# A weighted sum of two expert outputs: the 8-token tile moved from the end to the start, the last store in two halves

## The chip, the cores and the metric

The kernel runs on one core of one Trainium2 chip. The metric is the device time of one execution in microseconds; the time of a kernel is the median of several executions. A profiled execution also has a span, from the first to the last instruction of the program that the profiler recorded.

The core's engines that matter here are VectorE (DVE in the profile), ScalarE (ACT) and SyncE (SP), each with its own instruction stream. Data moves between HBM and the on-chip memory (128 partitions) by 16 DMA engines. A DMA is issued by SP or by ACT; the profile shows the two queues as q1 (SP) and q10 (ACT). Each of the 16 engines takes its share of every DMA, and a DMA has landed when all of them have reported.

## The reference

For 16 x 1024 tokens there are two expert outputs of 512 float32 each, and two weights. The result is their weighted sum.

```python
batch, seq, hidden, n_experts, k = 16, 1024, 512, 8, 2
expert_outputs: (batch, seq, k, hidden) float32      # 67.1 MB
combine_weights: (batch, seq, k) float32             # 0.13 MB

weights = combine_weights[..., np.newaxis]
return np.sum(expert_outputs * weights, axis=2)      # (batch, seq, hidden), 33.6 MB
```

## The kernel before

The 16384 tokens are dealt to the 128 partitions, 128 tokens to each (`per`). They are handled in 11 tiles: ten of J = 12 tokens per partition and a last one of LAST = 8. The helper `rows` (L34 to L38) splits the token axis into two blocks. In the first, each partition owns 120 tokens that lie one after the other in HBM, so that its rows start 480 KB apart in the input. In the second, each partition owns 8 tokens, with rows 32 KB apart (4 KB a token). `eo`, `cw` and `o` are functions that give the input, the weights and the output of `c` tokens from token `t` on.

All weights stay on chip in `wt`, loaded by two DMAs on ACT's queue (L54 to L57): 120 tokens first, then 8. An activation on a constant (L60) loads ACT's table early.

The loop (L62) goes over the 11 tiles. Each takes one of four buffers `et` of 12 tokens x 2 x 512 float32 per partition, 48 KB. The result `ot` (L65) lies in the first half of the same buffer, so a buffer is free for a later load once its store has landed. Loads (L69) are all issued by SP, one DMA per tile. Tile 0 alone is loaded in two pieces, 2 tokens and then the rest, the first of them in rows of 4 KB.

There are three kinds of tiles:

- Tiles 0 to 8: one product on DVE over both experts with the weights broadcast (L78), one sum on DVE (L79), and a store of 12 tokens issued by ACT (L80).
- Tile 9: ACT scales the first expert's half token by token (L86), DVE multiplies the second expert's half at once (L101) and adds (L102). SP issues the store (L103).
- Tile 10, the one of 8 tokens: for each token ACT scales the first expert's half (L86) and DVE multiplies and adds the second one's (L90), so that the two engines go hand in hand. SP issues the store of all 8 tokens (L103).

No semaphore is written by hand. A framework finds the dependencies between instructions from the parts of the tiles that they touch, sets the waits, and decides on the order of each engine's instructions. In the trace of before, SP issues the load of tile 10 at 194.63 us, ahead of the store of tile 9 at 218.73 us, though the loop names them the other way round.

Of the kernel before, what the change touches and what calls it, by code (L numbers as in the profile page):

```python
# [1 line left out]

# [4 lines left out]


@with_exitstack
def kernel(  # L10
    ctx: ExitStack,
    tc: tile.TileContext,
    expert_outputs: bass.AP,
    combine_weights: bass.AP,
    out: bass.AP,
):

    nc = tc.nc  # L20
    b, s, k, h = expert_outputs.shape
    assert k == 2
    n = b * s
    P = nc.NUM_PARTITIONS
    per = n // P
    assert per * P == n
    J, LAST = 12, 8
    main = per - LAST
    assert main % J == 0
    eo = expert_outputs.rearrange("b s k h -> (b s) (k h)")  # L30
    cw = combine_weights.rearrange("b s k -> (b s) k")
    o = out.rearrange("b s h -> (b s) h")

    def rows(x):  # L34

        a = x[0 : P * main, :].rearrange("(p t) f -> p t f", p=P)
        b = x[P * main : n, :].rearrange("(p t) f -> p t f", p=P)
        return lambda t, c: a[:, t : t + c, :] if t < main else b[:, t - main : t - main + c, :]  # L38

    eo, cw, o = rows(eo), rows(cw), rows(o)  # L40

    dt = mybir.dt.float32
    mult = mybir.AluOpType.mult
    add = mybir.AluOpType.add
    copy = mybir.ActivationFunctionType.Copy

    last = main // J

    wpool = ctx.enter_context(tc.tile_pool(name="w", bufs=1))
    ipool = ctx.enter_context(tc.tile_pool(name="in", bufs=4))  # L50

    wt = wpool.tile([P, per * k], dt)

    for t, c in ((0, main), (main, LAST)):  # L54
        nc.scalar.dma_start(
            out=wt[:, k * t : k * (t + c)].rearrange("p (t k) -> p t k", k=k), in_=cw(t, c)
        )  # L57

    warm = wpool.tile([P, 1], dt)
    nc.scalar.activation(out=warm, in_=nc.const_aps.tensor(1.0, (P, 1), dt), func=copy)  # L60

    for g in range(last + 1):  # L62
        et = ipool.tile([P, J, k * h], dt)

        ot = et.rearrange("p j f -> p (j f)")[:, 0 : J * h].rearrange("p (j f) -> p j f", f=h)  # L65
        t0, c = g * J, J if g < last else LAST

        for a, m in ((0, 2), (2, c - 2)) if g == 0 else ((0, c),):
            nc.sync.dma_start(  # L69
                out=et[:, a : a + m],  # L70
                in_=eo(t0 + a, m),
                max_dma_last_dim=k * h * 4 if g + a == 0 else None,
            )
        if g < last - 1:

            wb = wt[:, g * J * k : (g + 1) * J * k].unsqueeze(2).to_broadcast([P, J * k, h])
            ek = et.rearrange("p j (k h) -> p (j k) h", k=k)
            nc.vector.tensor_tensor(out=ek, in0=ek, in1=wb, op=mult)  # L78
            nc.vector.tensor_tensor(out=ot, in0=et[:, :, 0:h], in1=et[:, :, h : 2 * h], op=add)  # L79
            nc.scalar.dma_start(out=o(t0, c), in_=ot)  # L80
            continue


        for i in range(c):
            t = t0 + i
            nc.scalar.activation(  # L86
                out=et[:, i, 0:h], in_=et[:, i, 0:h], func=copy, scale=wt[:, 2 * t : 2 * t + 1]
            )
            if g == last:
                nc.vector.scalar_tensor_tensor(  # L90
                    out=ot[:, i, :],
                    in0=et[:, i, h : 2 * h],
                    scalar=wt[:, 2 * t + 1 : 2 * t + 2],
                    in1=et[:, i, 0:h],
                    op0=mult,
                    op1=add,
                )
        if g < last:
            w1 = wt.rearrange("p (t k) -> p t k", k=k)[:, t0 : t0 + c, 1:2]
            x1 = et[:, :, h : 2 * h]  # L100
            nc.vector.tensor_tensor(out=x1, in0=x1, in1=w1.to_broadcast([P, c, h]), op=mult)  # L101
            nc.vector.tensor_tensor(out=ot, in0=et[:, :, 0:h], in1=x1, op=add)  # L102
        nc.sync.dma_start(out=o(t0, c), in_=ot[:, 0:c])  # L103


# [1 line left out]
_INS = ['expert_outputs', 'combine_weights']  # L107
_OUTS = [((16, 1024, 512), 'float32')]


# [23 lines left out]
```

## Time and profile before

| | us |
|---|---|
| median of 5 runs | 239.1 |
| lowest and highest of the runs | 239.02, 240.06 |
| the profiled execution | 239.86 |
| its span | 238.1 |
| DVE busy | 194.0 (81% of the span) |
| ACT busy | 14.0 (6%) |

HBM is read for 67.24 MB and written for 33.55 MB, 423 GB/s over the span. The main groups of instructions (line, engine, operation, tiles, shapes, count | busy us, mean ns of one | idle time of the engine just before them, with what ended it):

```profile
L78 DVE TENSOR_TENSOR et<-et,wt 128x12288 f32<-128x12288 f32 x9 | 116.6, 12956 | 26.8 <-DMA et<-in_expert_outputs_dram 26.8
L79 DVE TENSOR_TENSOR et<-et 128x6144 f32<-128x6144 f32 x9 | 59.0, 6558 | 0.3
L86 ACT ACTIVATE et<-et,wt 128x512 f32<-128x512 f32 x20 | 12.5, 709 | 211.0 <-DMA et<-in_expert_outputs_dram 211.0
L90 DVE SCALAR_TENSOR_TENSOR et<-et,wt 128x512 f32<-128x512 f32 x8 | 5.6, 746 | 3.9 <-ACT et L86 3.7
```

The first line reads: line 78 ran nine times on VectorE, 12.956 us each; before these instructions VectorE was idle for 26.8 us in all, and each of those waits was ended by a load. The idle time of ACT is that of an engine with work in the last two tiles only.

The DMA issues (tiles, issuing queue, count, KB each, median us from issue to landing):

```profile
et<-in_expert_outputs_dram SPq DMA_DIRECT2D x9, 6144.0 KB, 31.7
out_dram<-et ACTq DMA_DIRECT2D x9, 3072.0 KB, 32.6
et<-in_expert_outputs_dram SPq DMA_DIRECT2D x1, 5120.0 KB, 16.8
et<-in_expert_outputs_dram SPq DMA_DIRECT2D x1, 4096.0 KB, 26.9
out_dram<-et SPq DMA_DIRECT2D x1, 3072.0 KB, 13.7
out_dram<-et SPq DMA_DIRECT2D x1, 2048.0 KB, 9.1
```

The time to landing holds the wait behind earlier transfers as well as the transfer.

### The profile page before, as it was taken

How to read it: one execution, taken by the hardware profiler on the slowest of the kernel's cores; microseconds unless marked ns; L12 is line 12 of the kernel's file. 1: busy time of each engine (PE TensorE's matmuls, PEld its weight loads, DVE VectorE, ACT ScalarE, POOL GpSimd, SP SyncE). 2: the span in 40 equal slices, each digit the busy share in tenths (PEclk: the TensorE clock that was granted, in tenths of full speed). 3: DMA queues.
4: the chain of work that ended last, by engine and by line, in shares of the span. 5: the costliest groups of instructions: out<-in, count | busy, mean ns of one | idle time of the engine just before them, and what ended most of it. 6: DMA issues, size and time to landing. Idle time of an engine off the chain costs nothing.

```text
span 238.1 us, 154 instructions
## 1 busy us (share of the span) xinstructions
DVE 194.0 (81%) x28; ACT 14.0 (6%) x22; POOL 0.2 (0%) x4
## 2 busy tenths in 40 slices
DVE  0009999999999999999699969969996999687630
ACT  2000000000000000000000000000000000660700
POOL 0000000000000000000000000000000000000000
DMA  8999999999999999999999999899999999999996
GB/s 308 441 463 396 396 529 392 392 446 413 405 396 462 438 417 458 401 516 405 462 396 405 429 429 504 351 462 396 524 396 462 396 405 454 399 462 434 405 428 259
DMA packets 3728, 100.80 MB, mean 423 GB/s; under 512 B 528, under 2 KB 656, under 8 KB 912
## 3 DMA queue, kind: packets, MB, share of 16 engines
q1 hardware_dynamic: 2144, 72.35, 70.7%
q10 hardware_dynamic: 1584, 28.44, 27.9%
HBM read 67.24 MB, written 33.55 MB: 423 GB/s over the span
## 4 chain that ended last, share of the span: by engine, by line
DMA 60%; DVE 33%; ACT 2%; DVEq 0%; ACTq 0%; issue 0%; SPq 0%
DMA et<-in_expert_outputs_dram 32%; DMA out_dram<-et 28%; DVE et L78 22%; DVE et L79 11%; ACT et L86 2%; DVE et L90 1%; DVEq L129 0%; ACTq L129 0%; SPq L69 0%; DVEq L78 0%; ACTq L86 0%
## 5 line engine op out<-in xcount | busy, mean ns | idle before, releaser
L78 DVE TENSOR_TENSOR et<-et,wt 128x12288 f32<-128x12288 f32 x9 | 116.6, 12956 | 26.8 <-DMA et<-in_expert_outputs_dram 26.8
L79 DVE TENSOR_TENSOR et<-et 128x6144 f32<-128x6144 f32 x9 | 59.0, 6558 | 0.3
L86 ACT ACTIVATE et<-et,wt 128x512 f32<-128x512 f32 x20 | 12.5, 709 | 211.0 <-DMA et<-in_expert_outputs_dram 211.0
L90 DVE SCALAR_TENSOR_TENSOR et<-et,wt 128x512 f32<-128x512 f32 x8 | 5.6, 746 | 3.9 <-ACT et L86 3.7
L101 DVE TENSOR_TENSOR et<-et,wt 128x6144 f32<-128x6144 f32 x1 | 6.6, 6557 | 2.3 <-DMA et<-in_expert_outputs_dram 2.3
L102 DVE TENSOR_TENSOR et<-et 128x6144 f32<-128x6144 f32 x1 | 6.6, 6557 | 0.9 <-ACT et L86 0.9
L60 ACT ACT_TABLE_LOAD x1 | 1.3, 1283 | 1.7 <-PEq L118 1.7
L60 ACT ACTIVATE warm<-const-float32-1.0 128x1 f32<-128x1 f32 x1 | 0.2, 204 | 0.0
L118 POOL MEMSET const-bfloat16-1.0<- 128x1 bf16 x1 | 0.1, 102 | 0.0
L118 POOL MEMSET const-uint8-127<- 128x1 uint8 x1 | 0.1, 102 | 0.0
L118 POOL MEMSET const-float32-0.0<- 128x1 f32 x1 | 0.1, 99 | 0.2 <-issue 0.2
L118 POOL MEMSET const-float32-1.0<- 128x1 f32 x1 | 0.1, 99 | 0.0
## 6 DMA issues: line engine op xcount, KB each, us to landing
et<-in_expert_outputs_dram SPq DMA_DIRECT2D x9, 6144.0 KB, 31.7
out_dram<-et ACTq DMA_DIRECT2D x9, 3072.0 KB, 32.6
et<-in_expert_outputs_dram SPq DMA_DIRECT2D x1, 5120.0 KB, 16.8
et<-in_expert_outputs_dram SPq DMA_DIRECT2D x1, 4096.0 KB, 26.9
out_dram<-et SPq DMA_DIRECT2D x1, 3072.0 KB, 13.7
out_dram<-et SPq DMA_DIRECT2D x1, 2048.0 KB, 9.1
et<-in_expert_outputs_dram SPq DMA_DIRECT2D x1, 1024.0 KB, 5.1
wt<-in_combine_weights_dram ACTq DMA_DIRECT2D x1, 120.0 KB, 3.2
```

Source lines behind the costliest of these rows:

```text
L60: nc.scalar.activation(out=warm, in_=nc.const_aps.tensor(1.0, (P, 1), dt), func=copy)
L78: nc.vector.tensor_tensor(out=ek, in0=ek, in1=wb, op=mult)
L79: nc.vector.tensor_tensor(out=ot, in0=et[:, :, 0:h], in1=et[:, :, h : 2 * h], op=add)
L86: nc.scalar.activation(out=et[:, i, 0:h], in_=et[:, i, 0:h], func=copy, scale=wt[:, 2 * t : 2 * t + 1])
L90: nc.vector.scalar_tensor_tensor(out=ot[:, i, :], in0=et[:, i, h : 2 * h], scalar=wt[:, 2 * t + 1 : 2 * t + 2], in1=et[:, i, 0:h], op0=mul ...
L101: nc.vector.tensor_tensor(out=x1, in0=x1, in1=w1.to_broadcast([P, c, h]), op=mult)
L102: nc.vector.tensor_tensor(out=ot, in0=et[:, :, 0:h], in1=x1, op=add)
L118: nc = _bacc.Bacc("TRN2", target_bir_lowering=False, num_devices=1)
```

## The change

The block of 8 tokens per partition comes first: it is the first 1024 tokens of the input in place of the last, and it is tile 0. Ten tiles of 12 tokens follow. Tile 0 is still loaded in two pieces, now of 2 and 6 tokens. Tiles 0 to 8 keep the two long DVE instructions, over 8 tokens in tile 0. Tile 9 stays as it was. Tile 10, which goes token by token, has 12 tokens, and its result is stored by two DMAs of 6 tokens each, both on SP. The weights of the 8 tokens are loaded ahead of the 120 others.

```diff
-    J, LAST = 12, 8
-    main = per - LAST
-    assert main % J == 0
+    J, FIRST = 12, 8
+    assert (per - FIRST) % J == 0
...
-        a = x[0 : P * main, :].rearrange("(p t) f -> p t f", p=P)
-        b = x[P * main : n, :].rearrange("(p t) f -> p t f", p=P)
-        return lambda t, c: a[:, t : t + c, :] if t < main else b[:, t - main : t - main + c, :]
+        a = x[0 : P * FIRST, :].rearrange("(p t) f -> p t f", p=P)
+        b = x[P * FIRST : n, :].rearrange("(p t) f -> p t f", p=P)
+        return lambda t, c: a[:, t : t + c, :] if t < FIRST else b[:, t - FIRST : t - FIRST + c, :]
...
-    last = main // J
+    last = (per - FIRST) // J
...
-    for t, c in ((0, main), (main, LAST)):
+    for t, c in ((0, FIRST), (FIRST, per - FIRST)):
...
-        t0, c = g * J, J if g < last else LAST
+        c = J if g else FIRST
+        t0 = FIRST + (g - 1) * J if g else 0
 
-        for a, m in ((0, 2), (2, c - 2)) if g == 0 else ((0, c),):
+        for a, m in ((0, c),) if g else ((0, 2), (2, c - 2)):
             nc.sync.dma_start(
                 out=et[:, a : a + m],
                 in_=eo(t0 + a, m),
-                max_dma_last_dim=k * h * 4 if g + a == 0 else None,
+                max_dma_last_dim=None if g + a else k * h * 4,
             )
         if g < last - 1:
-
-            wb = wt[:, g * J * k : (g + 1) * J * k].unsqueeze(2).to_broadcast([P, J * k, h])
-            ek = et.rearrange("p j (k h) -> p (j k) h", k=k)
+            wb = wt[:, t0 * k : (t0 + c) * k].unsqueeze(2).to_broadcast([P, c * k, h])
+            ek = et[:, 0:c].rearrange("p j (k h) -> p (j k) h", k=k)
             nc.vector.tensor_tensor(out=ek, in0=ek, in1=wb, op=mult)
-            nc.vector.tensor_tensor(out=ot, in0=et[:, :, 0:h], in1=et[:, :, h : 2 * h], op=add)
-            nc.scalar.dma_start(out=o(t0, c), in_=ot)
+            nc.vector.tensor_tensor(
+                out=ot[:, 0:c], in0=et[:, 0:c, 0:h], in1=et[:, 0:c, h : 2 * h], op=add
+            )
+            nc.scalar.dma_start(out=o(t0, c), in_=ot[:, 0:c])
             continue
...
-        nc.sync.dma_start(out=o(t0, c), in_=ot[:, 0:c])
+        for a, m in ((0, c),) if g < last else ((0, c // 2), (c // 2, c // 2)):
+            nc.sync.dma_start(out=o(t0 + a, m), in_=ot[:, a : a + m])
```

## The prediction

> **What bounds the kernel now.** I read the slices first, then the queues, the order of time, and stretches of the tail. The page's second part is the whole answer in two lines (40 slices of 5.95 us; tenths of the 16 DMA engines, then GB/s):
>
> ```profile
> DMA  8999999999999999999999999899999999999996
> GB/s 308 441 463 396 396 529 392 392 446 413 405 396 462 438 417 458 401 516 405 462 396 405 429 429 504 351 462 396 524 396 462 396 405 454 399 462 434 405 428 259
> ```
>
> Only the first and the last slice are not full. The queues' shares say the same:
>
> ```profile
> q1 hardware_dynamic: 2144, 72.35, 70.7%
> q10 hardware_dynamic: 1584, 28.44, 27.9%
> ```
>
> Together 98.6% of 238.1 us, so 234.8 us of the span the engines move bytes and 3.3 us they don't. The chain of waits gives DVE a third of the span, but that is the early part, where DVE had work piled up while the DMA engines were just as full; no byte waited for it. From 117 us on DVE is idle before each tile until its load lands. In order of time (start, duration, instruction, idle before):
>
> ```profile
> 117.57 12.96 DVE L78 TENSOR_TENSOR et<-et,wt 128x12288 f32<-128x12288 f32 x1 [2.04 <-DMA et<-in_expert_outputs_dram]
> ...
> 139.34 12.96 DVE L78 TENSOR_TENSOR et<-et,wt 128x12288 f32<-128x12288 f32 x1 [2.22 <-DMA et<-in_expert_outputs_dram]
> ...
> 161.11 12.96 DVE L78 TENSOR_TENSOR et<-et,wt 128x12288 f32<-128x12288 f32 x1 [2.22 <-DMA et<-in_expert_outputs_dram]
> ```
>
> The period is 21.77 us for one load and one store of 12 tokens (6144 + 3072 KB, 9.437 MB), 433.5 GB/s. That is my price for bytes: 14.51 us for a load of 12 tokens alone, 9.68 for one of 8; 7.26 for a store of 12 tokens, 4.84 for 8, 3.63 for a half of 12. At that price the 100.8 MB cost 232.5 us, begun at about 2.0 us.
>
> The tail, first the instructions, then stretches (bounds, length, busy of DVE, ACT, POOL, clock, DMA share, GB/s):
>
> ```profile
> 218.73 9.77 SPq L103 DMA_DIRECT2D out_dram<-et  x2
> 221.60 5.01 ACT L86 ACTIVATE et<-et,wt 128x512 f32<-128x512 f32 x8 [9.49 <-DMA et<-in_expert_outputs_dram]
> 222.36 5.77 DVE L90 SCALAR_TENSOR_TENSOR et<-et,wt 128x512 f32<-128x512 f32 x8 [3.65 <-ACT et L86]
> ```
>
> ```profile
> 204.00:212.00 8.00, 6.56 (x1) 7.35 (x12) 0.00 (x0) 1.00 1.06 459
> 212.00:218.70 6.70, 6.55 (x1) 0.11 (x1) 0.00 (x0) 1.00 0.95 411
> 218.70:221.50 2.80, 0.00 (x1) 0.00 (x0) 0.00 (x0) 1.00 0.99 424
> 221.50:228.40 6.90, 5.56 (x8) 5.01 (x8) 0.00 (x0) 1.00 1.04 449
> 228.40:232.40 4.00, 0.00 (x0) 0.00 (x0) 0.00 (x0) 1.00 0.94 403
> 232.40:236.00 3.60, 0.00 (x0) 0.00 (x0) 0.00 (x0) 1.00 0.86 369
> 236.00:238.10 2.10, 0.00 (x0) 0.00 (x0) 0.00 (x0) 1.00 0.02 8
> ```
>
> The last load lands at 221.52 and the last store is issued 6.6 us later, yet the engines stay full: tiles 8 and 9 have stores waiting in the queues, and they cover the last tile's arithmetic. This cover is the quantity that decides the case.
>
> **The change, part by part.** *Bytes.* None is added or taken: 11 loads, 11 stores' worth, two weight loads. Price 0, as long as no DMA engine idles where it didn't.
>
> *Eight tokens first.* Tile 0's load ends at 18.00 now (the chain of waits has it there); 2 MB less at 433.5 GB/s make it 13.2. Its product is 12.957 x 8/12 = 8.64 us, its sum 6.558 x 8/12 = 4.37, so its store goes out at about 26.3 in place of 37.72. Tile 1 lands at 13.2 + 14.5 = 27.7 and DVE waits 1.4 us for it. The engines are full of loads meanwhile (the four buffers would take 23 MB of them, 53 us), so 11.4 us earlier on the store is worth 0: it changes the order of the bytes. Buffer 0 comes free sooner, so the fifth load is issued some 14 us sooner, behind others in its queue: 0.
>
> *The weight loads* are as many, with 8 KB ahead of 120 KB. The 120 KB now travel beside tile 0's load. In the trace the engines are under-used between 2.2 and 3.0 us, while the 120 KB travel ahead; at most 0.3 us can be won there, and at most 0.3 lost by having them later, since 0.12 MB cost 0.28. I take 0.
>
> *SP and ACT queues.* SP issues the ten later loads, then tile 9's store, then two stores where there was one: one DMA issue more (0.35 us by L103's issues), behind a wait that it would not have delayed. Nothing is queued on SP behind the last store. ACT gets 4 more activations in the last tile (12 x 0.709 = 8.5 us), and DVE 4 more L90.
>
> *The last tile, 12 tokens in two stores.* L90 starts 0.84 us after the landing (221.52 to 222.36) and takes 5.77/8 = 0.721 per token. Let X be the landing of the last load. The sixth token ends at X + 0.84 + 6 x 0.721 = X + 5.17, the twelfth at X + 9.49; the halves are issued at X + 5.2 and X + 9.55. What covers them? X is the time of the slowest of 16 engines: by the landing records of the last load now, 15 engines were through at 219.4 to 219.7 and the last at 221.52. Call Y = X - 2.1 the time of the 15. At Y there remain tile 9's store (7.26 us) and a rest r of tile 8's. For r: both queues with work alternate packet by packet, one load's and one store's, hence the common period. The first store's packets begin 3.7 us after its issue now (37.72 to 41.44 by the packets' records); from 26.3 that is 30.0, when tile 2's load, begun at 27.3, is 1.5 of its 8 packets per engine ahead (1.81 us each). Stores then pair with loads one for one, so the loads stay 1.5 packets ahead, 2.3 if tile 1's store comes late (issued 47.3, wanted at 30.0 + 8 x (1.81 + 0.605) = 49.3, with 3.7 to start). So r is 1.5 to 2.3 of 8 packets of tile 8's store, 1.4 to 2.1 us; I take 1.7. The cover is 1.7 + 7.3 = 9.0 us, until Y + 9.0.
>
> From issue to first bytes takes 1.3 us at the kernel's start (issued 0.73, bytes from 2.0) and 3.7 for that first store, whose engines were busy. In the tail the engines run dry, so the near row is the start's. First half: Y + 7.3 + 1.3 = Y + 8.6, 0.4 us inside the cover: no gap. It lasts until Y + 12.6. Second half: Y + 11.65 + 1.3 = Y + 12.95: a gap of 0.35. By the other end, 3.7, the first half starts at Y + 11.0 (gap 2.0) and the second at Y + 15.35 (gap 0.7): 2.7 us. With r = 2.1 and 1.3 no gap is left. So 0 to 2.7, taken as 0.35; and since the slowest engine, which ends the kernel, is behind the others and has less or no gap, I put 0.2 on the end.
>
> *The end of the last store.* Now the other engines are done about 0.9 us before the last (the final 2.1 us hold almost no bytes). Smaller last packets may shorten this: between -0.9 and 0, taken as 0, since the order of packets on that engine doesn't change in kind.
>
> *The 32 KB pitch at the front.* Now loads of this pitch run from about 203 to 219 us, where the stretches above show 459 and 411 GB/s, mean 437: no price. In the first tile the pieces are 2 and 6 tokens of such rows, which no row shows; between 0 and, if it ran at the 308 GB/s of the first slice, 4.19 MB/308 - 9.68 = 3.9 us. I take 0, the row of the same pitch. The Trainium skill has a rule against such pitches ("DMA: Bandwidth & Descriptors", Latency and other measured facts): copies with per-partition pitches of large powers of two slow down, from 512 KiB on in its table, to half at 4 MiB. By its 512 KiB figure (207 against 214) tile 0's load would be an estimated 0.3 us dearer, by its worst one 10 us; 32 KB is below the table, and the stretches above show no loss.
>
> The sum: 0 + 0 + 0.2 + 0. The profiled execution, 238.1 us of span, took 239.86 in all, 1.76 around the span and 0.76 above the median of 239.1; the difference is what I carry over. Span 238.3, **time 239.3 us**.
>
> **Rivals.** *The cover is short* (slower). Place: after tile 9's store in the last 15 us. If a store needs over about 1.9 us from issue to bytes, both halves leave gaps that exceed 0.72 us together: at 2.5 us, the first half begins at Y + 9.8 (0.8), the second at Y + 14.15 (0.7), so +1.5: 240.6. For it: 12 tokens of arithmetic stand where 8 stood, and the first store's 3.7. Against it: that 3.7 contains waiting for busy engines, and the slowest engine has 2 us more of cover.
>
> *The halves don't part*: if the first store waits for all 12 tokens, 3 MB start at Y + 12.95, a gap of 3.95 us: 243. Against it: L90 already starts after one activation of a tile in which eight are to come, so waits follow parts of a tile.
>
> *The order on SP turns*: the last load behind the wait of tile 9's store, issued near 216 in place of 180; the engines would stand idle from about 208, tile 8's store being done, to 217: +9 or more, 248. Now SP puts that load (194.63) ahead of the store (218.73).
>
> *A tidier end* (faster): the 0.9 us of the last engine go, and 0.1 at the start: 238.1. For it: packets at the end are a quarter smaller. Against it: the lag of one engine is in nearly every load's landing.
>
> *A slow pitch at the front*: up to 3.9 us, 243.
>
> **How the numbers follow.** A measurement of this kernel tells 0.3%, 0.72 us, from no change. No change, by my sum: 0.47, with its own range 238.5 to 239.8. Short cover 0.28; halves not parted 0.03; order 0.02; pitch 0.02: slower 0.35. Tidier end: faster 0.18. The range takes in the gain of 0.9 to 1.0 and a cover short by most of the 2.7: 238.0 to 241.4; beyond it lie the three dear rivals and what is left of the short cover.
>
> **What would show it.** Slices of DMA at 9 from the second to the last but one; the first store issued near 26; DVE idle 1 to 2 us before every tile from the second on; the last L90 9.5 us after the last load; the stretch between that landing and the last store's issue above 400 GB/s. I am wrong if that stretch falls under 380, if the two last stores are issued together, or if the shares of the queues, near 234.8 us together, change by more than 0.7 us.

## The result and the profile after

The changed kernel takes 240.5 us in the median of 32 executions (239.35 to 241.33), the kernel before 239.1 (56 executions, 238.99 to 240.62). The ratio is 1.0042, with a 95% interval from 1.0032 to 1.0052: slower by 0.4%. The median moved further (1.4 us) than the ratio (1.0 us), because both kernels have executions in two places about a microsecond apart, a lower group with spans near 237.3 us and an upper one near 238.4, and the change moved most executions from the lower group to the upper one. The spans of the executions show it:

```
                     executions   span, median   span of 238.0 us or more   time minus span
before                   87           237.3              28                      1.78 to 1.80
changed                  32           238.4              26                      2.04
```

(The 87 are the executions of the kernel before that ran beside the experiments below.) So the 1.4 us of the median are 1.1 us of span and 0.26 us outside it. The profiled execution of the kernel before, 239.86 us, was one of the upper group. That of the changed kernel has 240.5 us, 238.4 of them span.

Slices and queues of the changed kernel (tenths of the DMA engines, GB/s; then packets, MB, share):

```profile
DMA  7999989999999999999999999999999999998996
GB/s 278 445 398 528 396 366 514 396 412 425 396 482 392 400 445 458 396 441 433 482 416 404 466 412 421 425 449 425 458 408 474 412 416 458 400 491 371 441 410 270
...
q1 hardware_dynamic: 2288, 73.40, 71.9%
q10 hardware_dynamic: 1584, 27.39, 26.8%
```

The engines are as full as before, 98.7% of the span. But 98.7% of 238.4 are 235.3 us for the same bytes; before they were 234.8 (235.2 and 234.7 by the records of the single packets). A packet is what one of the 16 engines moves at a time, here 48 KB of a load of 12 tokens or 24 KB of its store. The start in order of time:

```profile
13.34 8.69 DVE L77 TENSOR_TENSOR et<-et,wt 128x8192 f32<-128x8192 f32 x1 [13.34 <-DMA et<-in_expert_outputs_dram]
22.07 4.42 DVE L78 TENSOR_TENSOR et<-et 128x4096 f32<-128x4096 f32 x1
26.52 150.27 ACTq L81 DMA_DIRECT2D out_dram<-et  x8
27.85 12.96 DVE L77 TENSOR_TENSOR et<-et,wt 128x12288 f32<-128x12288 f32 x1 [1.36 <-DMA et<-in_expert_outputs_dram]
40.84 6.56 DVE L78 TENSOR_TENSOR et<-et 128x6144 f32<-128x6144 f32 x1
```

Tile 0's load is there at 13.2, its store goes out at 26.52, tile 1's at 47.4. The tail:

```profile
214.47 17.03 SPq L104 DMA_DIRECT2D out_dram<-et  x3
221.96 7.46 ACT L86 ACTIVATE et<-et,wt 128x512 f32<-128x512 f32 x12 [14.11 <-DMA et<-in_expert_outputs_dram]
222.72 8.43 DVE L90 SCALAR_TENSOR_TENSOR et<-et,wt 128x512 f32<-128x512 f32 x12 [8.28 <-ACT et L86]
```

```profile
218.70:221.90 3.20, 0.00 (x0) 0.00 (x0) 0.00 (x0) 1.00 1.07 461
221.90:227.10 5.20, 4.17 (x7) 5.14 (x9) 0.00 (x0) 1.00 1.01 435
227.10:231.20 4.10, 4.04 (x7) 2.32 (x4) 0.00 (x0) 1.00 0.93 399
231.20:234.00 2.80, 0.00 (x0) 0.00 (x0) 0.00 (x0) 1.00 1.02 434
234.00:236.00 2.00, 0.00 (x0) 0.00 (x0) 0.00 (x0) 1.00 0.96 412
```

From the landing of the last load (221.9) over the last token (231.15) to 236 the engines are full in every stretch. No gap opened in the tail. The time was not lost where the change does most to the program.

### The profile page after: what moved, and what is told of

The parts are those of the page before. It is cut to its first block, busy times and chain, and to the rows that moved or that the text cites. A ratio compares the mean times of both kernels' runs of the same rounds, so it can differ in the third digit from the quotient of the medians.

```text
span 238.4 us, 167 instructions
## 1 busy us (share of the span) xinstructions
DVE 190.5 (80%) x32; ACT 16.4 (7%) x26; POOL 0.2 (0%) x4
## 4 chain that ended last, share of the span: by engine, by line
DMA 68%; DVE 26%; ACT 2%; SPq 0%; issue 0%; DVEq 0%; ACTq 0%
DMA et<-in_expert_outputs_dram 44%; DMA out_dram<-et 23%; DVE et L77 16%; DVE et L78 8%; DVE et L90 2%; ACT et L86 2%; SPq L69 0%; DVEq L130 0%; ACTq L130 0%; DVEq L77 0%; ACTq L86 0%
## 5 line engine op out<-in xcount | busy, mean ns | idle before, releaser
L77 DVE TENSOR_TENSOR et<-et,wt 128x12288 f32<-128x12288 f32 (+1 forms) x9 | 112.4, 12484 | 28.7 <-DMA et<-in_expert_outputs_dram 28.7
L78 DVE TENSOR_TENSOR et<-et 128x6144 f32<-128x6144 f32 (+1 forms) x9 | 56.9, 6321 | 0.3
L86 ACT ACTIVATE et<-et,wt 128x512 f32<-128x512 f32 x24 | 14.9, 707 | 211.3 <-DMA et<-in_expert_outputs_dram 211.3
L90 DVE SCALAR_TENSOR_TENSOR et<-et,wt 128x512 f32<-128x512 f32 x12 | 8.2, 746 | 8.5 <-ACT et L86 8.3
L102 DVE TENSOR_TENSOR et<-et 128x6144 f32<-128x6144 f32 x1 | 6.6, 6559 | 0.9 <-ACT et L86 0.9
```

The costliest lines, as they stand in the source:

```text
L78: nc.vector.tensor_tensor(out=ot[:, 0:c], in0=et[:, 0:c, 0:h], in1=et[:, 0:c, h : 2 * h], op=add)
L86: nc.scalar.activation(out=et[:, i, 0:h], in_=et[:, i, 0:h], func=copy, scale=wt[:, 2 * t : 2 * t + 1])
L90: nc.vector.scalar_tensor_tensor(out=ot[:, i, :], in0=et[:, i, h : 2 * h], scalar=wt[:, 2 * t + 1 : 2 * t + 2], in1=et[:, i, 0:h], op0=mul ...
```

## The experiments

Each was run against the kernel before on the same chip. Ratios carry a 95% interval.

**The kernel before again.**

> The kernel before, once more, for its own trace and its spread. Its executions so far lie near 239.05 us (three quarters) or near 240.1 (a quarter). Both theories: ratio 1.000, within 0.002. If the two places come from when one of the 16 DMA engines ends, a trace of an execution near 239.05 shows the last store landing near 236.4, with all engines within 0.4 us, where the trace near 240 shows 237.3 with one engine 0.9 us behind.

239.1 us, ratio 1.0002 (0.9978 to 1.0025); 4 of 12 executions in the upper group. Its profiled execution (240.09) was of the upper group too. In both profiled ones the records of the landings show what the group is. The load of tile 2, the one under way when the first store sets in, is reported by 15 engines by 50.4 to 50.5 us and by the last at 52.2 to 52.4. One engine is then a load packet (1.8 to 1.9 us) behind in every later load, and the last store lands at 237.3 to 237.5, 0.9 to 1.0 us after the other engines. In profiled executions of the lower group (three kernels below with the same start) all engines report tile 2's load within 0.5 us and the last store within 0.5 us, at 236.5. So the two places are one engine's lag, and the first store's packets show where it is set. In the two profiled executions of the upper group one engine takes its first packet of that store at 41.4 to 41.5 us and the other 15 at 43.2 to 43.7, one load packet later; in those of the lower group all 16 take it at 43.1 to 43.8. By these counts, an engine that lets the store in a turn sooner is a load packet behind from then on. Why one does so in one execution and not in the next stays open.

**The 8 tokens first, the last store whole.**

```diff
-        for a, m in ((0, c),) if g < last else ((0, c // 2), (c // 2, c // 2)):
+        for a, m in ((0, c),):
```

> The change with the last store left whole, 12 tokens in one DMA. Theory A (the loss of about 1 us lies at the start, where the stores set in earlier): same as the changed kernel plus what the whole store exposes, by the cover of my prediction: first bytes at Y + 12.95 against a cover to Y + 9.0, about 4 us more, 243 to 244. Theory B (the loss comes from the second DMA of the last store): as the kernel before in its start, so only the 4 us: 242 to 243. If the stores in the queues cover more than I worked out, it is under 242.

241.91 us, ratio 1.0105 (1.0063 to 1.0147); spans of 238.8 to 239.0 in three executions and 240.7 to 241.0 in three. The profiled one (span 239.0) shows the exposed wait:

```profile
220.00:227.00 7.00, 5.70 (x9) 6.66 (x11) 0.00 (x0) 1.00 0.99 428
227.00:228.50 1.50, 1.50 (x3) 0.80 (x2) 0.00 (x0) 1.00 0.84 360
228.50:231.00 2.50, 1.02 (x2) 0.00 (x0) 0.00 (x0) 1.00 0.37 157
231.00:236.00 5.00, 0.00 (x0) 0.00 (x0) 0.00 (x0) 1.00 1.06 452
```

At 228.5 the stores in the queue are used up, and the engines are mostly idle until the whole store begins near 230.4. The gap is 1.65 us by the packets' records, where I had worked out 3.95: in this execution no engine lagged, so the load was in 1.7 us sooner against the cover than I assumed, and the store's first bytes came 0.9 us after its issue (229.55), not 1.3. The two halves are needed, and they do what they are for. The two groups are here 1.9 us apart, not 1. Probably the lag of the last load (1.8 us) counts whole where nothing covers the arithmetic; no execution of the upper group was profiled here. Without its gap the profiled span would be 237.4, that of the lower group, although the start is the changed kernel's.

**The kernel before with its last store in two halves**, run twice.

```diff
-        nc.sync.dma_start(out=o(t0, c), in_=ot[:, 0:c])
+        for a, m in ((0, c),) if g < last else ((0, c // 2), (c // 2, c // 2)):
+            nc.sync.dma_start(out=o(t0 + a, m), in_=ot[:, a : a + m])
```

> The kernel before with its last store of 8 tokens in two of 4. Theory A (loss at the start): 239.1, ratio 1.000. Theory B (one more DMA at the end costs): about 240, ratio 1.003 to 1.005. A third possibility, that halves help when the tile is short: 238.5, since the smaller last packets let the last engine end sooner.

> The kernel before with its last store of 8 tokens in two halves, a second time: twelve executions lay within 239.09 to 239.18, with none of those near 240.1 of which the kernel before has a quarter. If the halves prevent them: again all below 239.3, ratio 0.998. If that was chance, since what sets an engine back happens near 42 us, long before: two to four of twelve near 240.

239.12 and 239.15 us, ratios 0.9986 (0.9969 to 1.0004) and 0.9995 (0.9974 to 1.0016). The first time none of 12 executions lay in the upper group, the second time 3 did: the first was chance. Where the store was covered, a second DMA in it costs nothing and buys nothing beyond the intervals (about 0.2%). Theory B is out.

**The 8-token tile in the middle.** The tile list is `(main, LAST) if g == 5 else ((g - (g > 5)) * J, J)`, with the two long instructions cut to the tile's tokens and the last tile's store in two halves.

> The 8-token tile is the sixth of eleven; the first tile and the last have 12 tokens, the last one is stored in two halves as in the changed kernel. Theory A (loss at the start): the start is that of the kernel before, so 239.1 to 239.4. Theory B (loss at the end, 12 tokens of arithmetic and two stores): as the changed kernel, 240.0 to 240.5.

241.9 us, ratio 1.011 (1.0075 to 1.0145). It doesn't answer its question: the framework put the small tile's product ahead of tile 4's sum on DVE, so that tile 4's store went out late, and later loads with it. A load came 8.00 us late for DVE:

```profile
181.66 12.96 DVE L78 TENSOR_TENSOR et<-et,wt 128x12288 f32<-128x12288 f32 x1 [8.00 <-DMA et<-in_expert_outputs_dram]
```

**The start of before, the end of the change.** The 8-token tile is the tenth, and the last tile has 12 tokens, stored in two halves:

```diff
-        t0, c = g * J, J if g < last else LAST
+        t0, c = (main, LAST) if g == last - 1 else ((g - (g == last)) * J, J)
...
```

> The start is that of the kernel before (12 tokens first); the 8-token tile is the tenth, and the last tile has 12 tokens, stored in two halves as in the changed kernel. Theory C (the cost is at the start): 239.1 to 239.4, about a quarter of the executions a microsecond higher. Theory F (12 tokens of arithmetic at the end make the last engine's lag count): 240.4 or more.

239.23 us, ratio 1.0002 (0.9982 to 1.0022); median span 237.45, 4 of 12 in the upper group, as before. The tail is that of the changed kernel, 12 tokens in 8.43 us and two stores after tile 9's:

```profile
213.42 16.05 SPq L104 DMA_DIRECT2D out_dram<-et  x3
219.94 7.46 ACT L86 ACTIVATE et<-et,wt 128x512 f32<-128x512 f32 x12 [16.77 <-DMA et<-in_expert_outputs_dram]
220.69 8.43 DVE L90 SCALAR_TENSOR_TENSOR et<-et,wt 128x512 f32<-128x512 f32 x12 [7.30 <-ACT et L86]
```

Theory F falls. Between the medians the end of the change costs 0.1 us (the ratio's interval allows 0.5), though tile 9's store, which covers the end, is here one of 8 tokens. So the cost lies in the start, and outside the span.

**Tiny instructions added to the kernel before.**

```diff
+    cold = wpool.tile([P, 1], dt)
+    nc.vector.memset(cold, 0.0)
+    for _ in range(4):
+        nc.scalar.activation(out=warm, in_=warm, func=copy)
+        nc.vector.tensor_tensor(out=cold, in0=cold, in1=cold, op=mult)
```

> The kernel before with five tiny DVE instructions (128x1) and four tiny ACT ones added at the start, when both engines are idle. Between the span and the time of an execution lie 1.78 us in the kernel before and in the kernel with two halves of 4 tokens, but 2.06 in the changed kernel and in the one with a whole last store. Theory E (the number of instructions sets that rest): 2.0 to 2.1 here, and the time 239.3 to 239.4. Otherwise 1.78 and 239.1.

239.37 us against 239.13; the ratio, 1.0008 (0.9988 to 1.0028), is spread by the two groups. The spans are those of before (237.35 in the median), and the rest outside the span is 2.02 us. In all runs that rest goes with ACT's instructions. By the profiled executions, with 37 or 50 instructions recorded on ACT, semaphores and DMA issues included, it is 1.78 to 1.79 us; with 54 (the changed kernel among them) 2.02 to 2.06; with 55 in one kernel 2.57; with 66 in another 2.19. DVE's number alone doesn't set it: the run with the start of before has six more on DVE, none more on ACT, and 1.78. So 0.26 us of the change's cost are most likely its four more activations, not their execution, which is covered. The count over all engines is not ruled out, since it fits too: up to 162 instructions in the runs with 1.78 and from 163 on in the others. More than the number must count, as 55 and 66 show.

**Three attempts at the start.** By the packets' records tile 0's store (q10) ends at 47.2 us in the changed kernel, and tile 1's begins at 52.5. In the steady state such a change of store takes 3.6 us, two load packets; here it takes 5.3, three. Theory C said that the stores' second joining does the harm. First attempt: tile 1's product and sum in two halves, each with its store, for an earlier second store.

```diff
+            for a, m in ((0, 6), (6, 6)) if g == 1 else ((0, c),):
...
```

> The changed kernel with tile 1 worked in two halves of 6 tokens, so that half a store is issued near 37.6 us, while tile 0's store still runs (it ends near 46.8 now, and the next store is issued at 47.4, with packets from 50.8: the store queue is empty for 4 us and joins a second time). Theory C (each time that a store stream joins running loads costs about 0.2 to 0.3 us and can put one engine a packet behind): median 239.5 to 239.8, few executions above 240.2. Theory D (the early first store or the 12 tokens at the end cost, not the second joining): as the changed kernel, 240.4 to 240.6.

242.22 us, ratio 1.0122 (1.0102 to 1.0143). The framework put both half-products ahead of both half-sums, so the first half-store was issued at 44.22, not near 37.6. The pause at 47 us is back to 3.6 us even so, but buffer 1 now comes free only when the second half-store lands, at 84.1. The load that waits for it is issued when the load ahead of it has just ended. DVE sees it 6.6 us late, and the engines are busy longer for the same bytes (98.5% of 239.6, 236.0 us):

```profile
112.57 12.96 DVE L79 TENSOR_TENSOR et<-et,wt 128x12288 f32<-128x12288 f32 x1 [6.60 <-DMA et<-in_expert_outputs_dram]
```

```profile
q1 hardware_dynamic: 2288, 73.40, 71.7%
q10 hardware_dynamic: 1728, 27.39, 26.8%
```

Second attempt: tile 0's store held by a dependency on tile 1's product.

```diff
...
+                if g == 1 and a == 0:
+                    x = held[:, 0, 0:1]
+                    nc.vector.scalar_tensor_tensor(
+                        out=x, in0=et[:, 0, 0:1], scalar=zero, in1=x, op0=mult, op1=add
+                    )
+                    nc.scalar.dma_start(out=o(0, FIRST), in_=held)
...
```

> The changed kernel with tile 0's store held until half of tile 1's product is done: issued near 34.4 us in place of 26.5, so that it ends near 57 and tile 1's store, issued at 47.4, follows it without an empty queue. DVE gets a split product and an instruction on 128x1 elements that adds 0 times an element of tile 1. ACT's instructions are those of the changed kernel. Theory C (the second joining of the stores, near 51 us, puts engines behind in most executions): most executions fall to 239.4 to 239.6, a quarter lies a microsecond higher, median 239.5. Theory G (something else of the 8-token start, as its order of tiles or weights): 240.5 as the changed kernel.

240.44 us, ratio 1.0044 (1.0029 to 1.0059), all 12 spans from 238.2 to 238.9. It missed its condition and decides nothing. Both halves of the product ran ahead of the small instruction, so the store was issued at 41.09 instead of 34.4 and landed at 62; the fifth load, which waits for it, was issued at 62.16, when the fourth had ended (60.3, by the packets' records):

```profile
40.85 0.21 DVE L85 SCALAR_TENSOR_TENSOR et<-et,zero 128x1 f32<-128x1 f32 x1
41.09 0.35 ACTq L88 DMA_DIRECT2D out_dram<-et  x1
...
62.16 0.33 SPq L72 DMA_DIRECT2D et<-in_expert_outputs_dram  x1
```

Third attempt: tile 1 worked like tile 9, with ACT scaling one half.

```diff
-        if g < last - 1:
+        if g < last - 1 and g != 1:
...
```

> The changed kernel with tile 1 worked as tile 9 is, ACT scaling one half: its store is issued near 43 in place of 47.4, before tile 0's ends (46.8), and the first store stays early (26.5). Theory C: spans mostly 237.3 to 237.6 (the changed kernel: 238.4), as in the run with the held store. Theory H (an early first store is itself what disturbs): spans near 238.4, while the held store cures it. By theory E, now ACT's instructions alone, the 12 more activations widen the rest outside the span from 2.06 to 2.5 or more, so the time is 239.8 to 240.2 by C.

240.13 us, ratio 1.0032 (1.0017 to 1.0047). Tile 1's store goes out at 41.93, 5.5 us sooner than in the changed kernel, the pause is 3.6 us, and the load queue stays supplied:

```profile
27.85 7.46 ACT L86 ACTIVATE et<-et,wt 128x512 f32<-128x512 f32 x12 [24.63 <-DMA et<-in_expert_outputs_dram]
27.86 6.56 DVE L101 TENSOR_TENSOR et<-et,wt 128x6144 f32<-128x6144 f32 x1 [1.35 <-DMA et<-in_expert_outputs_dram]
35.34 6.56 DVE L102 TENSOR_TENSOR et<-et 128x6144 f32<-128x6144 f32 x1 [0.92 <-ACT et L86]
41.93 0.35 ACTq L104 DMA_DIRECT2D out_dram<-et  x1
```

This is the cleanest of the three. Eleven of 12 spans lie between 237.6 and 238.0 and one at 238.7; of the changed kernel's 32, 25 lie at 238.2 or above. The rest outside the span is 2.2 us, with 12 more activations. So the late second store is most likely what sends most executions of the changed kernel to the upper group, and the earlier one is worth 0.45 us of the 1.1 in the median span. It is not the only thing that differs: buffer 1 also comes free sooner, so the load that waits for it is issued at 71.39 instead of 73.33. Theory H falls as it was put: the first store is as early here. But the spans did not come back to 237.3 either; about 0.6 us remain that this kernel doesn't explain. Its profiled execution (span 237.7) shows no engine out of step at the start: the engines report each load within 0.55 us of each other up to 199 us, and only the last one, after tile 8's store has joined (issued at 199.61), over 1.35 us.

**The store queue left empty once in the kernel before**, by the same kind of dependency, on tile 1's store.

> The kernel before with tile 1's store held until after tile 2's product (issued near 70 in place of 57), so that the store queue is empty from about 64 to 73 and joins a second time; one DVE instruction on 128x1 elements adds 0 times an element of tile 2 to one of tile 1's result to force this. The bytes and the loads are the same and the loads' queue stays full. Theory C: the lower place of the executions rises by 0.2 to 0.3 and more of them lie a microsecond higher, median 240. Theory D: 239.1.

239.56 us, ratio 1.0011 (0.9989 to 1.0034), spans from 237.2 to 239.7 (leaving out one of 241.1). The executions do not lie in two groups, but the lower ones are as low as before, and in the profiled one no packet takes longer at the second joining. Here too the held store made a load late (a pause of 7.4 us in the load queue near 88 us). Inconclusive: an empty store queue doesn't cost a fixed price.

**An attempt to beat both**: two halves at the end, and tile 9 on DVE alone.

```diff
-        if g < last - 1:
+        if g < last:
...
```

> The kernel before with the last store in two halves and tile 9 worked by DVE alone like the tiles ahead of it, which takes 12 activations from ACT; its store is issued near 222.5 in place of 217 to 219 and is still covered by tile 8's until about 225.8. Theory E for ACT (its instruction count sets the rest outside the span: 50 recorded, 1.785 us; 54, 2.02 to 2.06; 55, 2.57): the rest falls below 1.78, to 1.2 to 1.6, and the time to 238.6 to 238.9. If 1.78 is a floor: 239.1. If the later store of tile 9 is not covered: 240 or more.

240.05 us, ratio 1.0041 (1.0019 to 1.0064). The rest outside the span stays at 1.78 with 37 instructions on ACT. Tile 9's store, issued at 222.38, was not covered as I had said:

```profile
220.00:224.00 4.00, 3.79 (x4) 4.00 (x7) 0.00 (x0) 1.00 1.25 455
224.00:226.00 2.00, 2.00 (x4) 0.76 (x2) 0.00 (x0) 1.00 0.51 221
226.00:232.00 6.00, 2.04 (x4) 0.00 (x0) 0.00 (x0) 1.00 0.96 412
```

A row counts a packet where it starts, so the 0.51 is not idle time. By the packets' records tile 8's store ends at 223.6, not 225.8, and the first packets of tile 9's store follow at once, but take 1.2 to 2.0 us instead of 0.91: 0.8 us per engine, which is about what the span lost (238.2 against 237.4).

No kernel here is shown to be faster than the one before.

## Why the prediction was right or wrong

The range held the time; the likeliest case, no change at 239.3, did not come. "Slower" had 0.35, but for another reason than the one that happened. So that the range held is luck: it was wide enough for a short cover, and the loss came at the start. The signs of being wrong did not catch it either: the two stretches ahead of the last store's issue held 435 and 399 GB/s, and the shares of the queues grew by 0.5 us, of the 0.7 named. Of the signs of being right one did not come: DVE did not wait before tile 2.

**What bounds it** was read rightly: the engines that move bytes are full, before and after.

**The start, timed rightly and priced wrongly.** Load at 13.2 (DVE began at 13.34), store at 26.3 (26.52), tile 1's load at 27.7 (DVE at 27.85), its store at 47.3 (47.4). The step that failed is "worth 0: it changes the order of the bytes". I had even noted that tile 1's store comes late against tile 0's, and used it for the tail alone. By the packets' records the same load packets take longer when the stores set in: together they cost about 0.7 us per engine near 39 to 47 us in the kernel before, and about 1.0 us in the changed one, in three places (29 to 31, 43.6, 53 to 56 us). The last place is the joining of tile 1's store; the kernel with the earlier second store doesn't have it, and its engines were busy for 234.9 us, not 235.2. What weighs more is that engines get out of step there: in the profiled execution of the changed kernel the landing of the last load is spread from 220.0 to 221.9 over the 16, in the run with the start of before from 219.4 to 219.85. The first packets of the store that joins tell which it will be (the records give the number of engines, not their names):

```
                                      first packets of the store that joins           loads afterwards
before, upper group, first store      1 engine at 41.4 to 41.5, 15 at 43.2 to 43.7    1 engine 1.8 to 1.9 us behind
start of before, lower, first store   16 at 43.1 to 43.8                              within 0.5 us
changed, second store                 5 at 50.8 to 51.0, 11 at 52.3 to 52.8           5 engines about 1 to 2 us behind
changed, last store whole, second     16 at 52.7 to 53.0                              within 0.4 us
earlier second store, second          16 at 50.5 to 51.0                              within 0.55 us, up to 199 us
```

So it is not the late joining as such that costs: in the kernel with the whole last store it is just as late, but all engines let the store in at the same turn, and no packet takes longer there. The first row stands for two profiled executions, the second for four, the others for one each. Together the start costs 1.1 us in the median span, as the run with the start of before shows by having none of it. The earlier second store returns 0.45; for the remainder no run here separates the first store's early joining from the rest of the new start.

**Around the span** I carried 1.76 us over. It is 2.04, with four more activations: 0.26 us that I had not thought of as a term (that the activations are the cause is likely, not shown). 1.1 and 0.26 make the 1.4 of the medians.

**The tail** was right. Cover, half-stores and arithmetic fit: L90 starts 0.84 us after the landing, the last token ends 9.3 after it, and no gap opened. The price was 0.2, and 0.1 was measured between medians. One reading in it was wrong: the 3.7 us from the first store's issue to its packets was taken from the one engine that let it in early (41.44). On the other 15 it was 5.6 to 5.8 us, and in the changed kernel 4.3 to 4.7 on all 16. The rest of tile 8's store that I counted as cover and the upper end of the range for the gaps were built on it. With 4.3 to 4.7 the loads are about two packets ahead when the stores begin, not 1.5, which is inside the range that I gave. The rival of a short cover is real only without the halves.

**The pitch** cost nothing: at full rate the load was to be there at 13.2, and DVE began at 13.34. The Trainium skill's rule on large power-of-two pitches ("DMA: Bandwidth & Descriptors", Latency and other measured facts) has a table that begins at 512 KiB; at the 32 KB of these rows no loss is seen here.

**The groups.** Five times were shown, and two of the five lay at 240. I took the median as the kernel's time and the profiled execution's 0.76 us as an offset to subtract. That offset was the upper group, and the change acts on how often it occurs.

## What to carry to other kernels

When a kernel is bound by its DMA engines, moving work around doesn't change the bytes, but it can change when a queue runs empty and joins again; look there, at the start and wherever a buffer comes free late, before calling a move free. Read the single times, not only their median: if they lie in groups, find in the landing records what sets a group, since a change may act on its frequency alone. Put the new end of a change on the old start; that separated this case in one run.

## What the runs showed of the hardware that was not expected

A load queue that runs empty for 6.6 to 6.7 us while stores go on cost about 0.8 us of engine time in the kernel with the held store and 1.2 in the one with two half-stores for tile 1, although the engines hardly idled (under 0.1 us): afterwards single load packets took up to 1.5 us longer than their usual 1.815. In the kernel before, held at one store, a pause of 7.4 us cost nothing in the one execution that was profiled, so this is no fixed price.

While loads run, the 16 engines need not let a store in at the same turn. The one that did so a load packet sooner than the other 15 was 1.8 to 1.9 us behind in every later load of the kernel before, and since a DMA has landed when the last engine reports, the compute engines saw each of these loads that much later.

The time outside the span is not constant. It went with the number of ACT's instructions: 1.78 us up to 50 recorded ones, 2.02 us or more from 54 on, 2.57 in one kernel with 55.
